# The output projection of a hybrid decoder layer by Strassen's algorithm, seven products of quarters instead of eight

## The chip, the core and the metric

The kernel runs on one core of a Trainium2 chip. The metric is the device time of one execution in microseconds (us). Within the core, TensorE (PE in the profile, its weight loads PEld) multiplies, VectorE (DVE), ScalarE (ACT) and GpSimd (POOL) do elementwise work, and the queue of SyncE (SP) issues every DMA of this kernel.

## What is computed

One decoder layer over 2048 tokens of width 2048: an input projection feeds a convolution branch and a windowed attention branch (each gated), their 1024 + 1024 channels are concatenated, and an output projection, a residual and a LayerNorm follow.

```python
proj = einsum("bsd,de->bse", x, w_in) + b_in
c_val, c_glu, c_gate, q, k, v, a_gate = split(proj)
y_conv = conformer_conv_branch(c_val, c_glu, ...) * silu(c_gate)   # GLU, causal conv of 31 taps, LayerNorm, swish
y_attn = swa_sink_attention(q, k, v, sinks) * silu(a_gate)         # window of 128, 16 heads, 2 kv heads
y = concatenate([y_conv, y_attn])
y = einsum("bse,ed->bsd", y, w_out) + b_out
out = layer_norm(2**0.25 * x + y, ln_g, ln_b)
```

All of it is float32. Each projection is made of three matmuls in a rounded 32-bit format: an operand is split into a rounded part (`hi`) and the remainder (`lo`), and `hi*hi + hi*lo + lo*hi` is summed (`mm3`).

## The kernel before

The tokens are worked in four chunks of 512 (`SC`, `NCH`). The body is one list of steps, 116 for each chunk: 8 "first" steps and 76 "in" steps (84 in all) for the input projection, with attention and convolution between them, then 32 "out" steps for the output projection. A step uses one weight tile of 128 x 1024 and gives PE 24 matmuls of 512 columns.

- Around each step, `load_w` fetches the raw weight tile three steps ahead (`wraw`, 3 buffers) and `split_w` splits it two steps ahead (`wspl`, 3 buffers): ACT makes `hi` (`copy`, L114), and `lo_part` (L117) makes the remainder on POOL for "in" steps and on DVE for "first" and "out" steps. A step's matmuls wait for both.
- Work of the convolution and of the LayerNorms waits in a deque (`bg`), from which `run_bg` takes some pieces in each step. At the first "out" step all that is left is run: the end of an inverse square root (`rsqrt_steps`) and eight `fin` pieces (L264 to L272), which make the convolution half of y.
- y is split into `hi` and `lo` where it is made: attention in pieces of 128 columns (`yah`, `yal`), the convolution in tiles of 512 (`ych`, `ycl`).
- An output column block `d` of 512 takes 8 steps. Four PSUM banks hold the four token rows of 128; `evac_out` adds each bank to the residual tile `xn` and feeds `bn_stats`. After the fourth block, `out_norm` queues 16 pieces for the final LayerNorm (ACT L435, DVE L436, POOL L437), which run in the next chunk's "first" steps. At the very end, `tail_norm` does it row by row.

A tile framework turns this into one instruction stream for each engine; it fills waiting time by its own estimate, so the order on an engine is not quite the order of the code. Each engine works its stream strictly in order.

Of the kernel before, what the change touches and what calls it, by code (L numbers as in the profile page):

```python
# [8 lines left out]
F32 = mybir.dt.float32  # L9
# [7 lines left out]
P = 128  # L17
# [13 lines left out]
NSLOT = 69  # L31
# [18 lines left out]
def hybrid_layer_kernel(ctx, tc, x, xT, w_first, w_in, w_out, consts, b_out, ln_g, ln_b, out):  # L50
# [9 lines left out]
    small = ctx.enter_context(tc.tile_pool(name="small", bufs=4))  # L60
    ps_acc = ctx.enter_context(tc.tile_pool(name="ps_acc", bufs=2, space=bass.MemoryType.PSUM))
# [87 lines left out]
    ys = {}  # L149
# [105 lines left out]
    def conv_var(c):  # L255
        ps = mean_bcast("vsplit", f"var{c}")
        v, y, tmp = slot(f"v{c}"), slot(f"rstd{c}"), slot(f"nt{c}")
        V.tensor_scalar(out=v, in0=ps, scalar1=EPS, scalar2=None, op0=ALU.add)
        bg.extend(rsqrt_steps(v, y, tmp))

        def fin(j):
            def f():
                a = st["conv", j]
                V.tensor_tensor(out=a, in0=a, in1=y, op=ALU.mult)  # L264
                u, t = half_silu_parts(a, half[:, 42 + j:43 + j], half[:, 50 + j:51 + j], f"cn{c}_{j}")
                silu_mul(u, u, t)
                bg_late.append((c, j, u))
                hi, lo = slot(f"ych{c}_{j}", F32R), slot(f"ycl{c}_{j}", F32R)
                V.tensor_tensor(out=u, in0=u, in1=st["gate", j], op=ALU.mult)
                copy(hi, u)  # L270
                lo_part(V, lo, u, hi)
                ys[c, 8 + j] = (hi, lo)  # L272
            return f
        bg_late = []
        bg.extend(fin(j) for j in range(8))
# [46 lines left out]
    def att_values(c, r, b):  # L322
        res = st.pop(("pm", r, b))
        pv = ps_pv.tile([P, 2, 256], F32, tag="pv", name=f"pv{c}_{r}_{b}")
        for kv in range(2):
            mv = slice(kv * 256, kv * 256 + 256)
            mm = []
            for n, (hi, lo) in enumerate(res):
                v = vt[:, b + 1 - n]
                mm.append((pv[:, kv, :], v[:, kv, :], hi[:, mv]))  # L330
                mm.append((pv[0:HD, kv, :], v[:, kv, 0:HD], lo[:, mv]))
            mm = [mm[0], mm[1], mm[3], mm[2]]
            for n, (o, l, m) in enumerate(mm):
                T.matmul(o, l, m, start=(n == 0), stop=(n == len(mm) - 1))  # L334

        o = small.tile([P, 2, P], F32, tag="o", name=f"o{c}_{r}_{b}")
        of = o.rearrange("p i q -> p (i q)")
        cols = slice(b * P, (b + 1) * P)
        for kv in range(2):
            rows, other = slice(kv * HD, (kv + 1) * HD), slice((1 - kv) * HD, (2 - kv) * HD)  # L340
            copy(of[rows], pv[other, kv, :])
            V.tensor_tensor(out=of[rows], in0=of[rows], in1=pv[rows, kv, :], op=ALU.add)
        for i in range(2):
            e = 2 * r + i
            if b == 0:
                ys[c, e] = (slot(f"yah{c}_{e}", F32R), slot(f"yal{c}_{e}", F32R))
            hi, lo = ys[c, e]
            V.tensor_tensor(out=o[:, i, :], in0=o[:, i, :], in1=st["ag", e][:, cols], op=ALU.mult)
            copy(hi[:, cols], o[:, i, :])
            lo_part(V, lo[:, cols], o[:, i, :], hi[:, cols])  # L350
# [56 lines left out]
    def evac_out(c, d, s, ps):  # L407
        z = st["z", c, s, d] = st["xn", s]
        V.tensor_tensor(out=z, in0=z, in1=ps, op=ALU.add)  # L409
        if d == 0:  # L410
            st["bn", c, s] = small.tile([P, 4, 6], F32, tag="bn", name=f"bn{c}_{s}", bufs=8)
        V.bn_stats(out=st["bn", c, s][:, d, :], in_=z)

# [29 lines left out]
    def out_norm(c):  # L443

        units = [(d, s) for d in range(4) for s in range(4)]

        def first():
            norm_small(c, range(4))
            load_gb(c, 0)

        def fin(n):
            def f():
                if n < 16:
                    d, s = units[n]
                    if s == 0 and d < 3:
                        load_gb(c, d + 1)
# [5 lines left out]
        return [first] + [fin(n) for n in range(18)]  # L462
# [3 lines left out]
    for c in range(NCH):  # L466
# [3 lines left out]
        for d in range(4):  # L470
            for p in range(8):
                steps.append(("out", c, d, p))
# [3 lines left out]
    def w_src(s):  # L476
        if s[0] == "first":
            return w_first[s[2]]
        return w_in[s[2] - 4, s[5]] if s[0] == "in" else w_out[s[2], s[3]]
# [10 lines left out]
    def split_w(n, parts=1, in_slots=False):  # L490
# [4 lines left out]
        eng = G if steps[n][0] == "in" else V  # L495
        if in_slots:
            hi, lo = ([slot(f"w{x}{n}_{i}", F32R) for i in range(2)] for x in "hl")
            parts = 2
        else:
            hi, lo = (wspl.tile([P, 1024], F32R, tag=f"w{x}", name=f"w{x}{n}") for x in "hl")  # L500
        for i in range(parts):
            w = slice(i * 1024 // parts, (i + 1) * 1024 // parts)
            h, l = (hi[i], lo[i]) if in_slots else (hi[:, w], lo[:, w])
            copy(h, t[:, w])
            lo_part(eng, l, t[:, w], h)
        splits[n] = (hi, lo) if in_slots else ((hi[:, 0:512], hi[:, 512:1024]), (lo[:, 0:512], lo[:, 512:1024]))
# [3 lines left out]
    per = 84 + 32  # L510
    for c in range(NCH):
# [10 lines left out]
        att.setdefault(base + 82, []).append((conv_var, c))  # L522

    ps = None

    def mm3(o, lh, ll, mh, ml, start, stop):
        T.matmul(o, lh, mh, start=start, stop=False)  # L527
        T.matmul(o, lh, ml, start=False, stop=False)  # L528
        T.matmul(o, ll, mh, start=False, stop=stop)  # L529

    def out_mm(c, n, p, i):
        hi, lo = splits[n]
        for kk in range(2):
            k = 2 * p + kk
            yh, yl = ys[c, k]
            cols = slice(i * P, (i + 1) * P)
            mm3(st["acc"][i], yh[:, cols], yl[:, cols], hi[kk], lo[kk], k == 0, k == KT - 1)
# [45 lines left out]
    split_x(0, 1)  # L583
    for n, s in enumerate(steps):
        c = s[1]
        tail = c == NCH - 1 and s[0] == "out" and s[2] == 3
        if c == 0 and s[0] == "first":
# [13 lines left out]
        elif tail:  # L601

            p = s[3]
            if p < 3:
                b = n - p
                if p == 0:
                    split_w(b + 2)
                for q in (2 * p + 3, 2 * p + 4):
                    if q < 8:
                        list(load_w(b + q))  # L610
                        split_w(b + q, in_slots=q < 5)
        else:
            list(load_w(n + 3))
            split_w(n + 2)
        for f, *args in att.get(n, []):
            f(*args)
        if s[0] == "first":
# [4 lines left out]
            for kk in range(2):  # L622
                k = 2 * p + kk
                xh, xl = xs[c, k]
                for t in range(4):
                    cols = slice(t * P, (t + 1) * P)
                    mm3(st["acc"][t], hi[kk][:, cols], lo[kk][:, cols], xh, xl, k == 0, k == KT - 1)
            if p == 7:
# [15 lines left out]
        else:  # L644
            _, c, d, p = s
            if d == 0 and p == 0:
                run_bg(len(bg))
            if p == 0:
                st["acc"] = four_banks(f"out{c}_{d}")
            if p == 2:  # L650
                st["bo"] = bcast_row(b_out, d, f"bo{c}_{d}")
            if 2 <= p < 6:
                xn = st["xn", p - 2] = slot(f"xn{c}_{d}_{p - 2}")
                r = c * SC + (p - 2) * P
                nc.sync.dma_start(out=xn, in_=x[r:r + P, d * 512:(d + 1) * 512])
            if 4 <= p:
                xn = st["xn", p - 4]
                V.scalar_tensor_tensor(out=xn, in0=xn, scalar=ALPHA, in1=st["bo"], op0=ALU.mult, op1=ALU.add)
            q = d * 8 + p
            if c + 1 < NCH and q >= 23:  # L660
                for k in (2 * (q - 23), 2 * (q - 23) + 1):
                    if k < KT:
                        load_x(c + 1, k)
                    if k >= 2:
                        split_x(c + 1, k - 2)
            if not tail:
                for i in range(4):
                    out_mm(c, n, p, i)
                if p == 7:
                    for i in range(4):  # L670
                        evac_out(c, d, i, st["acc"][i])
                    if d == 3:
                        bg.extend(out_norm(c))
            elif p < 3:
                for i in range(4):
                    out_mm(c, n, p, i)
            elif p == 7:
                for d2 in range(4):
                    load_gb(c, d2)
                for i in range(4):  # L680
                    for q in range(3, 8):
                        out_mm(c, n - 7 + q, q, i)
                    evac_out(c, d, i, st["acc"][i])
                    tail_norm(c, i)
        if not tail:
# [68 lines left out]
```

## Time and profile before

| | |
|---|---|
| median of 3 runs | 2746.8 us (2745.5 to 2747.04) |
| profiled execution | 2745.35 us, its span 2743.6 us |
| PE busy | 2696.2 us, 12448 matmuls |
| DVE / ACT / POOL busy | 1952.4 / 1120.5 / 1118.7 us |
| DMA | 308.53 MB, mean 112 GB/s |

The span is from the first instruction to the last. Matmuls overlap in the records: one of 512 columns shows about 390 ns, but the next starts about 227 ns later, and it is that distance that counts. The same holds in small for other engines. In rows of the timeline the first two numbers are the start and the length in us; in groups, "x304 | 746.7, 2459" means 304 instructions, 746.7 us together, 2459 ns for one on average.

### The profile page before, as it was taken

The page shows a single profiled execution, that of the slowest core. Times are in us where ns is not written, and L with a number is a line of the kernel's source. Part 1 is how long each engine was busy: PE and PEld are TensorE (multiplying, and loading weights), DVE is VectorE, ACT ScalarE, POOL GpSimd, SP SyncE. Part 2 cuts the span into 40 slices and gives each one's busy share as a digit, 9 for nine tenths or more (in the row PEclk, how much of TensorE's full clock was granted, in tenths as well). Part 3 has the DMA queues.
Part 4 walks back from the last instruction along what each step waited for, and adds up shares of the span by engine and source line. Part 5 has one row for each costly group of instructions (what it writes and reads, how often), then busy time and mean ns, then how long its engine had stood idle before and what let it go on. Part 6 is the DMA issues. An engine that isn't in the chain of part 4 may idle for free.

```text
span 2743.6 us, 33348 instructions
## 1 busy us (share of the span) xinstructions
PE 2696.2 (98%) x12448; PEld 2243.1 (82%) x12448; DVE 1952.4 (71%) x2986; ACT 1120.5 (41%) x2060; POOL 1118.7 (41%) x632
## 2 busy tenths in 40 slices
PE   9999999999999999999999999999999999999996
PEld 7888888888788888878878888887887888888885
DVE  5587877754857887775585779777457677986827
ACT  4344454522434445442243443544233345444422
POOL 2455555200645555610064555560006455556002
PEclk9999999999999999999999999999999999999998
DMA  5222222364422222235442222224544222222424
GB/s 179 96 89 85 79 91 92 100 208 145 148 91 92 85 78 93 85 129 189 142 153 87 90 77 85 92 86 147 171 150 146 85 92 85 77 92 86 158 99 142
DMA packets 101826, 308.53 MB, mean 112 GB/s; under 512 B 11296, under 2 KB 11424, under 8 KB 101664
## 3 DMA queue, kind: packets, MB, share of 16 engines
q1 hardware_dynamic: 101664, 306.40, 33.2%
q8 instruction: 98, 1.61, 0.2%
q14 instruction: 64, 0.52, 0.1%
HBM read 289.58 MB, written 16.78 MB: 112 GB/s over the span
## 4 chain that ended last, share of the span: by engine, by line
PE 90%; DVE 4%; issue 2%; ACT 2%; POOL 1%; DMA 1%; SPq 0%; DVEq 0%; POOLq 0%
PE in L529 21%; PE in L527 21%; PE in L528 21%; PE out L527 7%; PE out L529 7%; PE out L528 7%; PE pv L334 2%; PE sc L284 1%; PE sc L285 1%; PE pt L311 1%; POOL vsum L248 1%; DMA xn<-in_x_dram 1%; DVE wl L117 1%; DVE xn L436 0%; DVE xn L565 0%
## 5 line engine op out<-in xcount | busy, mean ns | idle before, releaser
L529 PE MATMUL in<-xh,wl 128*128 128x512 f32 x2688 | 1050.3, 391 | 10.9 <-DVE wl L117 10.9
L527 PE MATMUL in<-xh,wh 128*128 128x512 f32 x2688 | 1053.8, 392 | 5.6 <-ACT xh L114 5.6
L528 PE MATMUL in<-xl,wh 128*128 128x512 f32 x2688 | 1049.5, 390 | 0.0
L117 POOL TENSOR_TENSOR wl<-wr,wh 128x1024 fp32r<-128x1024 f32 x304 | 746.7, 2459 | 637.6 <-ACT wh L114 602.9
L114 ACT ACTIVATE wh<-wr 128x1024 fp32r<-128x1024 f32 (+1 forms) x467 | 488.6, 1050 | 824.8 <-PE out L529 345.8
L203 DVE SCALAR_TENSOR_TENSOR cv<-h,cst,cv 128x512 f32<-128x512 f32 x896 | 632.1, 746 | 2.3
L529 PEld LDWEIGHTS in<-xh,wl 128*128 128x128 f32 x2688 | 505.8, 188 | 119.1 <-DVE wl L117 12.6
L527 PEld LDWEIGHTS in<-xh,wh 128*128 128x128 f32 x2688 | 506.5, 188 | 106.2 <-ACT xh L114 5.6
L528 PEld LDWEIGHTS in<-xl,wh 128*128 128x128 f32 x2688 | 506.1, 188 | 101.6 <-DVE xl L117 0.5
L117 DVE TENSOR_TENSOR wl<-wr,wh 128x1024 fp32r<-128x1024 f32 (+1 forms) x163 | 214.1, 1316 | 255.3 <-ACT wh L114 250.7
L437 POOL TENSOR_TENSOR xn<-xn,b 128x512 f32<-128x512 f32 x48 | 85.8, 1819 | 582.9 <-DVE xn L436 582.9
L527 PE MATMUL out<-wh,yah 128*128 128x512 f32 x512 | 199.7, 391 | 4.0 <-DVE xn L409 4.0
L528 PE MATMUL out<-wl,yah 128*128 128x512 f32 x512 | 199.3, 389 | 0.0
L527 PE MATMUL out<-wh,ych 128*128 128x512 f32 x512 | 199.2, 389 | 0.0
L528 PE MATMUL out<-wl,ych 128*128 128x512 f32 x512 | 199.2, 389 | 0.0
L529 PE MATMUL out<-wh,ycl 128*128 128x512 f32 x512 | 199.2, 389 | 0.0
L529 PE MATMUL out<-wh,yal 128*128 128x512 f32 x512 | 198.6, 389 | 0.0
L299 ACT ACTIVATE pr<-pr,sm 128x128 f32<-128x128 f32 x256 | 99.8, 391 | 165.9 <-DVE sm L295 165.9
L527 PEld LDWEIGHTS out<-wh,yah 128*128 128x128 f32 x512 | 96.1, 188 | 27.1 <-DVE xn L409 6.3
L529 PEld LDWEIGHTS out<-wh,yal 128*128 128x128 f32 x512 | 96.1, 188 | 20.1
L529 PEld LDWEIGHTS out<-wh,ycl 128*128 128x128 f32 x512 | 96.1, 188 | 20.0
L527 PEld LDWEIGHTS out<-wh,ych 128*128 128x128 f32 x512 | 96.1, 188 | 20.0
(281 smaller groups left out, 2877.3 us busy)
## 6 DMA issues: line engine op xcount, KB each, us to landing
wr<-in_w_in_dram SPq DMA_DIRECT2D x304, 512.0 KB, 3.2
wr<-in_w_out_dram SPq DMA_DIRECT2D x128, 512.0 KB, 3.3
xr<-in_xT_dram SPq DMA_DIRECT2D x64, 256.0 KB, 4.1
xn<-in_x_dram SPq DMA_DIRECT2D x64, 256.0 KB, 5.8
out_dram<-xn SPq DMA_DIRECT2D x64, 256.0 KB, 2.1
wr<-in_w_first_dram SPq DMA_DIRECT2D x31, 512.0 KB, 3.7
bo<-in_b_out_dram SPq DMA_DIRECT2D x16, 256.0 KB, 5.9
g<-in_ln_g_dram SPq DMA_DIRECT2D x16, 256.0 KB, 5.4
```

What stands on the lines that cost most here:

```text
L114: A.activation(out=dst, in_=src, func=AF.Copy)
L117: eng.tensor_tensor(out=dst, in0=src, in1=hi.bitcast(F32), op=ALU.subtract)
L203: V.scalar_tensor_tensor(out=o, in0=h[:, t:t + SC], scalar=wt(t), in1=a, op0=ALU.mult, op1=ALU.add)
L248: G.tensor_tensor(out=s, in0=st["vsum"], in1=q, op=ALU.add)
L284: T.matmul(o, qs[:, b * P:(b + 1) * P], ks[kv][:, b * P:b * P + 256], start=True, stop=False)
L285: T.matmul(o, qs[:, b * P:(b + 1) * P], kl[kv][:, b * P:b * P + 256], start=False, stop=True)
L299: A.activation(out=p3[:, u, :], in_=p3[:, u, :], func=AF.Exp, scale=HD ** -0.5, bias=sm[:, 1, u:u + 1], accum_out=sm[:, 3, u:u + 1])
L334: T.matmul(o, l, m, start=(n == 0), stop=(n == len(mm) - 1))
L437: G.tensor_tensor(out=z, in0=z, in1=st["b", d], op=ALU.add)
L527: T.matmul(o, lh, mh, start=start, stop=False)
L528: T.matmul(o, lh, ml, start=False, stop=False)
L529: T.matmul(o, ll, mh, start=False, stop=stop)
```

## The change

The output projection of a chunk, 512 tokens x 2048 channels x 2048 columns, is cut into quarters (256 tokens, 1024 channels, 1024 columns; a is the attention half of y, b the convolution half) and done with seven products instead of eight, in the order `PRODS`. Each product takes 8 steps (two column blocks `dp`, four weight tiles `p`), so an "out" part has 56 steps instead of 32, but a step multiplies only 256 tokens, so it has 12 matmuls instead of 24.

```diff
-NSLOT = 69
+NSLOT = 63
+PRODS = (1, 2, 5, 6, 3, 7, 4)
-    wraw = ctx.enter_context(tc.tile_pool(name="wraw", bufs=3))
-    wspl = ctx.enter_context(tc.tile_pool(name="wspl", bufs=3))
+    wraw = ctx.enter_context(tc.tile_pool(name="wraw", bufs=4))
+    wspl = ctx.enter_context(tc.tile_pool(name="wspl", bufs=4))
...
+    def gen_y(c, i, k):
+        a, b = yr.get((c, k)), yr.get((c, 8 + k))
+        h1, h2 = slice(0, 256), slice(256, 512)
...
+        if i == 1:
+            src = a[:, h1]
+        elif i == 2:
+            src = b[:, h1]
+        elif i == 4:
+            src = b[:, h2]
+        elif i == 5:
+            G.tensor_tensor(out=sm, in0=a[:, h2], in1=b[:, h2], op=ALU.add)
+        elif i == 6:
+            G.tensor_tensor(out=sm, in0=sm, in1=a[:, h1], op=ALU.subtract)
+        elif i == 3:
+            G.tensor_tensor(out=sm, in0=b[:, h1], in1=sm, op=ALU.subtract)
+        else:
+            G.tensor_tensor(out=a[:, h1], in0=a[:, h1], in1=a[:, h2], op=ALU.subtract)
...
+        copy(t[:, 0, :], src)
+        lo_part(V, t[:, 1, :], src, t[:, 0, :])
...
+    def tsum_add(dp, p, kk):
+        b11, b12, b21, b22 = st["tb", dp, p, kk]
+        G.tensor_tensor(out=b11, in0=b12, in1=b11, op=ALU.subtract)
+        G.tensor_tensor(out=b12, in0=b22, in1=b12, op=ALU.subtract)
+        G.tensor_tensor(out=b22, in0=b22, in1=b11, op=ALU.subtract)
+        G.tensor_tensor(out=b21, in0=b21, in1=b22, op=ALU.subtract)
...
     def split_w(n, parts=1):
-        eng = G if steps[n][0] == "in" else V
+        eng = G if steps[n][0] == "in" or steps[n][0] == "out" and steps[n][4] % 2 else V
...
+    for j in range(16):
+        job = (j // 8, j // 2 % 4, j % 2)
+        att.setdefault(10 + 4 * j, []).append((tsum_load, *job))
+        att.setdefault(14 + 4 * j, []).append((tsum_add, *job))
+        att.setdefault(18 + 4 * j, []).append((tsum_store, *job))
...
-            list(load_w(n + 3))
-            split_w(n + 2)
+            list(load_w(n + 4))
+            split_w(n + 3)
...
+            if q == 0:
+                while len(bg) > 8:
+                    run_bg(1)
+                out_banks(c)
+            if i == 1 and dp == 0:
+                gen_y(c, 1, 4 + p)
...
+            out_mm(n, i, dp, p, (0,) if tail else (0, 1))
...
+            if p == 3 and not tail:
+                late = [(evac_out, c, i, dp, tp) for tp in range(2)]
+            if i == 1:
+                run_bg(1)
+            if i != 4:
+                gen_y(c, PRODS[PRODS.index(i) + 1], 4 * dp + p)
+            if q == 40:
+                bg.extend(out_norm(c, (0, 1)))
+            if q > 40 and not tail:
+                run_bg(1)
```

In the changed file `copy` is L117, `lo_part` L120, `fin` L268 to L272, `scale_xn` L410, `add_bank` L413, `bn_stats` L420, the four sums of `gen_y` L466 to L475, the LayerNorm pieces L531 to L533. In detail:

- **y** is kept unsplit (`yr`), and `gen_y` makes the operand of the next product one tile of 256 columns at a time: 56 tiles in a chunk, 32 of them with a sum on POOL first, each with a copy on ACT and a remainder on DVE. The splits of 128 columns in the attention are gone.
- **Weight sums**: four of the seven products need a sum of weight quarters. In the first chunk's "in" part, 16 jobs load weights, form the sums on POOL (64 subtractions of 512 columns) and store them in DRAM, from where all chunks load them as they load weights.
- **Weight splits** in the "out" part: 56 instead of 32 in a chunk, the remainder on DVE for even `p` and on POOL for odd `p`. Loads are issued four steps ahead, splits run three ahead, with four buffers each.
- **Banks**: two sets of four PSUM banks (X, the ones attention uses, and Z) take turns; every product is added to one output quarter when it is done, so there are 28 additions of a bank in a chunk (16 before), one product running on in its bank.
- **LayerNorm**: rows 0 and 1 are done from the sixth product on, rows 2 and 3 in the next chunk's "first" steps. At the end, only rows 2 and 3 go through `tail_norm`.

Where instructions stand now: on POOL, around the first chunk's "out" part (`wl` is a weight remainder, the number behind it the step, of which 84 is the first "out" step; `vsum` belongs to the convolution's LayerNorm, `xn` with `b` to the final one of the next "first" steps). Before:

```order
L248 TENSOR_TENSOR vsum0_5_4215<-vsum0_4_4175,sq0_5_4213 128x512
L248 TENSOR_TENSOR vsum0_6_4220<-vsum0_5_4215,sq0_6_4218 128x512
L248 TENSOR_TENSOR vsum0_7_4225<-vsum0_6_4220,sq0_7_4223 128x512
L117 TENSOR_TENSOR wl83_4265<-wr83_4231,wh83_4264 128x1024
L437 TENSOR_TENSOR xn0_0_0_4544<-xn0_0_0_4544,b0_0_5694 128x512
```

POOL goes from the last "in" weight straight to the LayerNorm of the next part. In the changed kernel, on POOL, from the split of out step 15 on (`S` are the sums for products 5, 6 and 3, `ya` that for 7):

```order
L120 TENSOR_TENSOR wl99_4976<-wr99_4951,wh99_4975 128x1024
L466 TENSOR_TENSOR S0_0_4901<-ya0_0_1241,cn0_0u_4649 128x256
L466 TENSOR_TENSOR S0_0_4901<-ya0_1_1243,cn0_1u_4682 128x256
L466 TENSOR_TENSOR S0_2_4946<-ya0_2_2140,cn0_2u_4714 128x256
L466 TENSOR_TENSOR S0_2_4946<-ya0_3_2142,cn0_3u_4746 128x256
L469 TENSOR_TENSOR S0_0_4901<-S0_0_4901,ya0_0_1241 128x256
L120 TENSOR_TENSOR wl101_5027<-wr101_5002,wh101_5026 128x1024
L466 TENSOR_TENSOR S0_4_4997<-ya0_4_2849,cn0_4u_4780 128x256
L466 TENSOR_TENSOR S0_4_4997<-ya0_5_2851,cn0_5u_4810 128x256
L469 TENSOR_TENSOR S0_0_4901<-S0_0_4901,ya0_1_1243 128x256
L469 TENSOR_TENSOR S0_2_4946<-S0_2_4946,ya0_2_2140 128x256
L469 TENSOR_TENSOR S0_2_4946<-S0_2_4946,ya0_3_2142 128x256
```

POOL now has work throughout the "out" part, and nearly all of its 32 sums stand between the splits of out steps 15 and 25, fourteen of them between those of steps 17 and 19 alone.

On DVE, in the stretch where the convolution half of y is made (`cn` the pieces of `fin`, `wl` the weight remainders). Before:

```order
L117 TENSOR_TENSOR ycl0_1_4408<-cn0_1u_4402,ych0_1_4407 128x512
L144 SCALAR_TENSOR_TENSOR cn0_2u_4413<-cn0_2t_4414,cn0_2u_4413 128x512
L269 TENSOR_TENSOR cn0_2u_4413<-cn0_2u_4413,cgate0_2u_3959 128x512
L117 TENSOR_TENSOR ycl0_2_4419<-cn0_2u_4413,ych0_2_4418 128x512
L117 TENSOR_TENSOR wl89_4573<-wr89_4536,wh89_4572 128x1024
L144 SCALAR_TENSOR_TENSOR cn0_3u_4424<-cn0_3t_4425,cn0_3u_4424 128x512
```

Now, at its end:

```order
L147 SCALAR_TENSOR_TENSOR cn0_7u_4868<-cn0_7t_4869,cn0_7u_4868 128x512
L271 TENSOR_TENSOR cn0_7u_4868<-cn0_7u_4868,cgate0_7u_4606 128x512
L120 TENSOR_TENSOR wl100_5005<-wr100_4973,wh100_5004 128x1024
L120 TENSOR_TENSOR y0_2_7_4874<-cn0_7u_4868,y0_2_7_4874 128x256
L120 TENSOR_TENSOR y0_5_0_4903<-S0_0_4901,y0_5_0_4903 128x256
L120 TENSOR_TENSOR y0_5_1_4925<-S0_0_4901,y0_5_1_4925 128x256
L413 TENSOR_TENSOR xn0_0_0_4634<-xn0_0_0_4634,out0_0_4883 128x512
```

The weight remainder of out step 16 (`wl100`) stands between the last pieces of the convolution, and right behind it DVE takes up the tiles that POOL's sums feed.

More of the change, by code (lines that the diff above doesn't have):

```diff
@@ L461, in fin @@
             return f
-        return [first] + [fin(n) for n in range(18)]
+        return [first] + [fin(n) for n in range(len(units) + 2)]
     steps = []
@@ L469, in hybrid_layer_kernel @@
             steps += [("in", c, t, *ORDER[t], hf) for hf in range(2)]
-        for d in range(4):
-            for p in range(8):
-                steps.append(("out", c, d, p))
+        steps += [("out", c, i, dp, p) for i in PRODS for dp in range(2) for p in range(4)]
     raws, splits = {}, {}
@@ L583, in hybrid_layer_kernel @@
     split_x(0, 1)
+    late = []
     for n, s in enumerate(steps):
         c = s[1]
-        tail = c == NCH - 1 and s[0] == "out" and s[2] == 3
         if c == 0 and s[0] == "first":
@@ L644, in hybrid_layer_kernel @@
         else:
[L645 to L684, printed above, removed]
@@ L685, in hybrid_layer_kernel @@
-        if not tail:
+            _, c, i, dp, p = s
+            q = 8 * PRODS.index(i) + 4 * dp + p
+            tail = c == NCH - 1 and q >= 52
+            if q == 0:
[4 more added lines that the diff above has]
+                gen_y(c, 1, 4 + p)
+            if i == 2 and dp == 0 and p == 0:
+                st["Z"] = four_banks(f"out{c}")
+            if i in NEW:
+                if p == 0:
+                    st["bo"] = bcast_row(b_out, NEW[i](dp, 0)[1], f"bo{c}_{i}_{dp}")
+                if p < 2:
+                    load_xn(c, *NEW[i](dp, p))
+                else:
+                    scale_xn(*NEW[i](dp, p - 2), st["bo"])
@@ new lines, in hybrid_layer_kernel @@
+            if c + 1 < NCH and q >= 39:
+                if q < 55:
+                    load_x(c + 1, q - 39)
+                if q >= 40:
+                    split_x(c + 1, q - 40)
+            if q == 55:
+                if not tail:
+                    bg.extend(out_norm(c, (2, 3)))
+                else:
+                    run_bg(len(bg))
+                    for d in range(4):
+                        load_gb(c, d)
+                    evac_out(c, i, dp, 0)
+                    tail_norm(c, 2)
+                    for pp in range(4):
+                        out_mm(n - 3 + pp, i, dp, pp, (1,))
+                    evac_out(c, i, dp, 1)
+                    tail_norm(c, 3)
@@ L686, in hybrid_layer_kernel @@
+        if not (s[0] == "out" and tail):
             raws.pop(n, None)
```

162 lines of the change are left out of this document (110 added, 52 removed).

## The prediction

> **What bounds the kernel now.** I read the page's busy shares first, then the chain that ended last.
>
> ```profile
> PE 2696.2 (98%) x12448; PEld 2243.1 (82%) x12448; DVE 1952.4 (71%) x2986; ACT 1120.5 (41%) x2060; POOL 1118.7 (41%) x632
> PE 90%; DVE 4%; issue 2%; ACT 2%; POOL 1%; DMA 1%; SPq 0%; DVEq 0%; POOLq 0%
> ```
>
> TensorE bounds it: 90% of the chain is its matmuls. Next the busy time by stage, to see who else works in the "out" parts; two of them, with the "in" part ahead of the first (the edges come from the PE timeline below):
>
> ```profile
> core 0: us, PE busy (x) PEld busy (x) DVE busy (x) ACT busy (x) POOL busy (x), PEclk, DMA share, GB/s
> 0.00:507.70 507.70, 500.57 (x2344) 417.88 (x2345) 367.86 (x589) 223.08 (x450) 257.75 (x161) 1.00 0.29 100
> 507.70:683.20 175.50, 174.62 (x769) 143.90 (x768) 100.93 (x132) 60.34 (x74) 0.00 (x0) 1.00 0.50 165
> 1186.80:1362.80 176.00, 175.19 (x773) 144.55 (x772) 101.48 (x133) 60.15 (x74) 0.00 (x0) 1.00 0.49 165
> ```
>
> An "out" part takes 175.5 us, PE is busy without a gap, DVE 101 us, and POOL does nothing at all. The timeline gives the matmul's pace:
>
> ```profile
> 507.73 0.39 PE L527 MATMUL out<-wh,yah 128*128 128x512 f32 x1
> 507.95 0.39 PE L528 MATMUL out<-wl,yah 128*128 128x512 f32 x1
> 683.02 0.39 PE L529 MATMUL out<-wh,ycl 128*128 128x512 f32 x1
> 683.25 0.39 PE L527 MATMUL in<-xh,wh 128*128 128x512 f32 x1
> ```
>
> From 507.73 to 683.25 it is 175.5 us for 768 matmuls, 0.228 each; a single distance is 0.227, which I use.
>
> **What is removed.** Seven products of 96 matmuls are 672 instead of 768 in a chunk: 96 x 0.227 = 21.8 us, 87 us in all four. The new "out" part could take 672 x 0.227 = 152.3 us. But a weight step now has 12 matmuls, 2.72 us, where it had 5.44, and each still needs its load, its copy on ACT and its remainder on DVE or POOL. So the question is whether the other engines can feed PE at twice the rate.
>
> **Prices of what is added.** From DVE's and POOL's timelines, each where the other engine was idle or on PSUM work:
>
> ```profile
> 505.52 1.22 DVE L117 TENSOR_TENSOR wl<-wr,wh 128x1024 fp32r<-128x1024 f32 x1
> 506.66 0.69 DVE L130 TENSOR_TENSOR nt<-nt,rstd 128x512 f32<-128x512 f32 x1
> 512.82 2.49 DVE L264 TENSOR_TENSOR conv<-conv,rstd 128x512 f32<-128x512 f32 x4
> 120.51 2.40 POOL L117 TENSOR_TENSOR wl<-wr,wh 128x1024 fp32r<-128x1024 f32 x1 [3.05 <-ACT wh L114]
> 128.80 1.31 POOL L117 TENSOR_TENSOR plu<-pmu,phu 128x512 fp32r<-128x512 f32 x1
> ```
>
> On DVE a remainder of 1024 columns takes 1.14 us from start to start, 512 columns 0.62; by that slope I estimate 0.35 for 256. POOL takes 2.40 and 1.30; by its slope 0.75 for 256. Busy time alone would fit: counting the changed "out" part of the first chunk in order, from behind the split of its first step to that of its last, DVE has 27 remainders of 1024, 70 operations of 512 with two inputs from SBUF and 56 of 256, so 30.8 + 43.4 + 19.6 = 93.8 us, and besides 36 operations on a bank or with one input (22 us by 0.62) and 18 small ones (3 us). POOL has 28 remainders, 32 sums and 8 LayerNorm additions: 67.2 + 24.0 + 10.4 = 101.6 us. ACT has 56 copies of 1024 by 1.05 us (row below), 56 of 256 that I put at 0.4 and some 30 others, about 100 us. Each is under 152.
>
> ```profile
> L114 ACT ACTIVATE wh<-wr 128x1024 fp32r<-128x1024 f32 (+1 forms) x467 | 488.6, 1050 | 824.8 <-PE out L529 345.8
> ```
>
> But DVE and POOL don't run side by side. The timeline of the LayerNorm behind the first "out" part, DVE first, then POOL, and two rows from a little earlier:
>
> ```profile
> 691.16 9.80 DVE L436 TENSOR_TENSOR xn<-xn,g 128x512 f32<-128x512 f32 x7
> 700.89 2.31 DVE L117 TENSOR_TENSOR wl<-wr,wh 128x1024 fp32r<-128x1024 f32 x1
> 703.12 9.16 DVE L436 TENSOR_TENSOR xn<-xn,g 128x512 f32<-128x512 f32 x6
> 712.20 2.28 DVE L117 TENSOR_TENSOR wl<-wr,wh 128x1024 fp32r<-128x1024 f32 x1
> 714.40 4.05 DVE L436 TENSOR_TENSOR xn<-xn,g 128x512 f32<-128x512 f32 x3
> 691.98 12.36 POOL L437 TENSOR_TENSOR xn<-xn,b 128x512 f32<-128x512 f32 x7 [192.82 <-DVE xn L436]
> 704.98 10.63 POOL L437 TENSOR_TENSOR xn<-xn,b 128x512 f32<-128x512 f32 x6 [0.63 <-DVE xn L436]
> 716.24 5.60 POOL L437 TENSOR_TENSOR xn<-xn,b 128x512 f32<-128x512 f32 x3 [0.63 <-DVE xn L436]
> 496.76 2.40 POOL L117 TENSOR_TENSOR wl<-wr,wh 128x1024 fp32r<-128x1024 f32 x1 [1.69 <-ACT wh L114]
> 497.66 2.58 DVE L117 TENSOR_TENSOR wl<-wr,wh 128x1024 fp32r<-128x1024 f32 x1 [1.20 <-ACT wh L114]
> ```
>
> The same DVE operation goes from 0.62 to 1.40 us, the remainder from 1.22 to 2.3, and POOL's addition from 1.30 to 1.77. From 691.16 to 718.4 (27.2 us) DVE did 16 x 0.62 + 2 x 1.14 = 12.2 us of work at its lone price and POOL about 14 additions, 18.4 us: together 30.6 in 27.2, a factor of 1.12 where two independent engines could reach 2. Near enough they take turns. Operations with one input in PSUM escape: the convolution's taps (L203) average 0.746 us although POOL is busy half of the "in" part.
>
> ```profile
> L203 DVE SCALAR_TENSOR_TENSOR cv<-h,cst,cv 128x512 f32<-128x512 f32 x896 | 632.1, 746 | 2.3
> 500.17 0.68 DVE L258 TENSOR_SCALAR v<-var 128x512 f32<-128x512 f32 x1
> ```
>
> **The "out" part, added up.** Where DVE's row above stands (500.17) the work counted here can begin, 7.6 us ahead of PE's first "out" matmul. At out step 25, behind POOL's block of sums, DVE must have done 12 remainders, 44 operations of 512 and 32 of 256 (13.7 + 27.3 + 11.2 = 52.2 us), POOL 13 remainders and all 32 sums (31.2 + 24.0 = 55.2): 107.4 / 1.12 - 7.6 = 88.3 us after PE's start, where PE alone would be there at 25 x 2.72 = 68.0. So PE comes 20.3 us late, and the part takes at least 152.3 + 20.3 = 172.6. At the last step the sum is (93.8 + 101.6) / 1.12 - 7.6 = 166.9 against 149.6, with DVE's other 25 us all hidden in POOL's turns; with none hidden 192.1, so 42.5 late and 194.8. I take 182, four tenths of the way: a third of that other work stands ahead of step 25, where POOL has a backlog to hide it; the rest doesn't, and the streams are in strict order. That is +6.5 us a chunk against 175.5, **+26** in all (-12 to +77): Strassen's 87 us are spent before they are earned.
>
> **The rest, part by part.**
>
> The LayerNorm moved: today its 16 pieces delay a "first" step's remainder, and PE waits in three of the four chunks. PE's rows, and its windows:
>
> ```profile
> 710.68 0.39 PE L528 MATMUL in<-xl,wh 128*128 128x512 f32 x1
> 714.53 0.73 PE L529 MATMUL in<-xh,wl 128*128 128x512 f32 x1 [3.47 <-DVE wl L117]
> 712.00:714.00 2.00, 0.00 (x0) 1.00 0.35 131
> 716.00:718.00 2.00, 2.00 (x6) 0.50 0.89 261
> PE in L529 <- DVE wl L117: 10.9, 4, 3.5
> ```
>
> 3.85 us without a matmul, then some seven at half the clock, about 5 us a time. Eight pieces instead of 16, and splits one step further ahead, should end much of it; but the backlog of the "out" part falls there. **-8** (-15 to 0).
>
> The tail: PE's last matmul and DVE's last chains of a row:
>
> ```profile
> 2722.16 0.39 PE L529 MATMUL out<-wh,ycl 128*128 128x512 f32 x1
> 2721.10 0.68 DVE L409 TENSOR_TENSOR xn<-xn,out 128x512 f32<-128x512 f32 x1
> 2730.47 0.67 DVE L409 TENSOR_TENSOR xn<-xn,out 128x512 f32<-128x512 f32 x1
> ```
>
> Now 21.2 us pass from PE's end to the span's end, since four rows pass through DVE at 9.4 us each. With two rows, the first starts 5.4 us (24 matmuls) before PE's end, the second 9.4 later, and it needs the 13.1 from 2730.47 to 2743.6: 17.1. **-4** (-6 to +1).
>
> The weight sums: 64 x 1.30 = 83 us of POOL in a part of 507.7 us where it is busy 257.75, so 67%. Their stores sit in SP's queue ahead of weight loads and wait for POOL, but loads run four steps, 21 us, ahead. **+2** (0 to +15).
>
> At nothing: the split of y taken out of the attention (it lies under the "in" matmuls, and the list of PE's waits doesn't name it), and the banks' changes of hands, since each is emptied three steps before its next product.
>
> DMA: an "out" part moves 56 x 0.524 MB of weights and 56 pieces of 0.262 MB (16 of the next chunk's x, 16 of the residual, 8 of the bias, 16 of the LayerNorm's factors and results), 44 MB. The busiest stretch of today:
>
> ```profile
> 544.00:564.00 20.00, 19.11 (x84) 15.35 (x83) 16.72 (x25) 4.05 (x5) 0.00 (x0) 1.00 0.92 299
> ```
>
> 299 GB/s at a share of 0.92 is 325 at most, so 44 MB need 135 us: hidden on average. In the last two products it is 18.4 MB, 57 us, against 43.5 of PE; since PE is late by then and half of these loads are not urgent, I add nothing and keep it as a rival.
>
> Sum: +26 - 8 - 4 + 2 = +16, so 2745.35 + 16 = **2761 us**. (That execution is 1.5 us under the median of the runs shown.)
>
> **Rivals.**
>
> *Faster: the turns matter less.* POOL's sums begin in gaps that the block count misses and DVE's bank work fills POOL's turns. If PE waits only for the convolution's last pieces, some 5 us, a part takes 158: 4 x (158 - 175.5) = -70, -10 as above: 2665. Half as good (168): -30 - 10: 2705. For it: two operations in 27 us do overlap, the rate is a mean. Against: the counts at step 25 leave no slack. It decides once a part ends less than 24 us late, under 176.5 us.
>
> *Slower: full exclusion.* If POOL's and DVE's operations exclude each other for their whole length, the last step comes at 195.4 - 7.6 = 187.8, 38 late, a part takes 190.5, and the sum is +60 - 10: 2795. For it: the two rows at 496.76, where the remainder on DVE ended 3.5 us after POOL's began, the sum of both alone. The Trainium skill states this as the rule ("SBUF — State Buffer", "Who interferes with whom"): the port pair shared by VectorE and GpSimd is an exclusive lock, held for the instruction, against DVE operations with two SBUF inputs; by it the total would be this rival's 2795. The LayerNorm rows above, with their 1.12, stand slightly better than that rule.
>
> *Slower: the clock.* Each wait as long as the 3.85 us above costs another 1.7 at half clock. If the 20 to 30 us of lateness come as five such waits in a part: +8.5 x 4 on the forecast: 2795.
>
> *Slower: DMA.* If the last two products run at 57 us instead of the forecast's 48: +36: 2797.
>
> **How the numbers follow.** Changes within 0.2% (5.5 us) can't be told from none. Forecast, 2751 to 2785: 0.25. Full exclusion 0.20, clock 0.07, DMA 0.05: slower 0.57. The faster rival as far as 2705: 0.20, beyond, to 2665: 0.15, so 0.35. Between them, unchanged: 0.08. The range leaves out about 0.12 below 2695 and 0.08 above 2835; the forecast's own range is 2712 to 2838 by the terms' bounds.
>
> **What would show it.** Right: "out" parts of 175 to 190 us; POOL busy over half of them; two-input DVE operations near 1.2 us where they took 0.69; PE waiting for a POOL remainder around out step 19 to 25. Wrong: parts near 155 us with PE gapless, or waits of PE on DMA. The step most likely to fail is the factor 1.12 and how much of DVE's other work it hides.

## The result, and the profile after

| | before | after |
|---|---|---|
| median (lowest to highest) | 2746.91 us (2745.5 to 2747.04) | 2817.57 us (2816.29 to 2821.37) |
| ratio, 95% interval | | 1.0261 (1.0243 to 1.0278): slower by 2.6% |
| profiled execution, its span | 2745.35, 2743.6 us | 2818.5, 2816.8 us |
| the four "out" parts (the last to PE's last matmul) | 175.5, 175.3, 176.3, 175.3 us | 199.8, 197.3, 199.0, 192.7 us |

The product has 384 matmuls less, and yet the kernel is 71 us slower. The page of after, its busy shares:

```profile
PE 2665.3 (95%) x12064; PEld 2183.6 (78%) x12064; DVE 2218.8 (79%) x3120; ACT 1242.2 (44%) x2220; POOL 1635.7 (58%) x938
```

PE's share fell from 98 to 95%: it waits now. The busy time of two "out" parts, in the columns of the prediction's rows:

```profile
508.80:708.60 199.80, 168.93 (x674) 130.44 (x673) 181.56 (x207) 98.80 (x148) 119.52 (x67) 0.95 0.63 213
1209.20:1406.50 197.30, 168.79 (x674) 131.26 (x673) 180.95 (x208) 99.67 (x148) 119.50 (x67) 0.94 0.64 217
```

DVE (third) is busy for 181.6 us of 199.8, so 91%. But by the prediction's count and its lone prices it had 93.8 + 25 = 118.8 us of work: by that estimate 63 us of its "busy" time are waiting inside instructions. POOL (fifth) had 101.6 us of work and shows 119.5, so it waits for 18. PE is fed by both. By shape in the same stretch, first DVE, then POOL (the last two numbers ahead of the second bar are the group's busy time and one operation's ns):

```profile
L120 DVE TENSOR_TENSOR wl<-wr,wh 128x1024 fp32r<-128x1024 f32 x27 | 41.1, 1523 | 2.2 <-ACT wh L117 2.2
L120 DVE TENSOR_TENSOR y<-S,y 128x256 fp32r<-128x256 f32 x24 | 24.2, 1032 | 1.8 <-ACT y L117 1.8
L532 DVE TENSOR_TENSOR xn<-xn,g 128x512 f32<-128x512 f32 x8 | 10.9, 1372 | 0.3 <-ACT xn L531 0.3
L420 DVE BATCH_NORM_STATS2 bn<-xn 128x6 f32<-128x512 f32 x14 | 9.0, 677 | 0.0
L413 DVE TENSOR_TENSOR xn<-xn,out 128x512 f32<-128x512 f32 x12 | 7.7, 676 | 0.6 <-PE out L629 0.6
L120 POOL TENSOR_TENSOR wl<-wr,wh 128x1024 fp32r<-128x1024 f32 x27 | 74.1, 2748 | 75.8 <-ACT wh L117 75.8
```

The pieces of y (256 columns, two inputs from SBUF) take 1032 ns on average, the sum with a bank (`xn<-xn,out`) and the statistics the usual 676. PE's waits, the five largest in the "out" parts:

```profile
PE out L628 <- POOL wl L120: 26.8, 11, 4.8
PE xb L628 <- DVE wl L120: 16.9, 15, 2.3
PE xa L627 <- ACT y L117: 16.1, 8, 3.6
PE xa L628 <- DVE wl L120: 10.5, 7, 2.8
PE xa L628 <- POOL wl L120: 10.2, 9, 2.4
```

The first row is the wait that the prediction placed near out step 19. Here it is on the timelines of PE, DVE and POOL:

```profile
578.46 0.39 PE L627 MATMUL out<-wh,y 128*128 128x512 f32 x1
583.65 0.50 PE L628 MATMUL out<-wl,y 128*128 128x512 f32 x1 [4.80 <-POOL wl L120]
584.68 0.63 PE L628 MATMUL out<-wl,y 128*128 128x512 f32 x1
587.25 0.55 PE L628 MATMUL out<-wl,y 128*128 128x512 f32 x1
579.66 1.74 DVE L120 TENSOR_TENSOR wl<-wr,wh 128x1024 fp32r<-128x1024 f32 x1
581.32 2.56 DVE L120 TENSOR_TENSOR y<-S,y 128x256 fp32r<-128x256 f32 x1
573.77 4.18 POOL L475 TENSOR_TENSOR ya<-ya 128x256 f32<-128x256 f32 x4
580.28 3.31 POOL L120 TENSOR_TENSOR wl<-wr,wh 128x1024 fp32r<-128x1024 f32 x1
```

POOL works off sums until 580, then its remainder takes 3.31 us instead of 2.40; DVE's remainder ends at 581.4, and from there on it is 2.2 us. DVE's next piece, 0.35 us by itself, takes 2.56: it ends at 583.9, 0.3 behind POOL's remainder. PE stands still for 5 us, and then its matmuls come 0.43 us apart until 587.6 instead of 0.227.

Lateness of PE, at some steps of the first "out" part, against 2.72 us a step from the part's first matmul (read from PE's timeline, which holds all 672 matmuls of this part, 12 a step):

| step | 8 | 16 | 24 | 32 | 40 | 48 | 54 |
|---|---|---|---|---|---|---|---|
| after | 9.8 | 16.0 | 27.8 | 33.6 | 33.6 | 43.5 | 47.4 |

It rises in two stretches: through the convolution's last pieces and the sums (to step 32), and again at the end, where the LayerNorm pieces run.

### The profile page after: what moved, and what is told of

It reads as the page before. It is cut to its first block, busy times and chain, and to the rows that moved or that the text cites. A ratio compares the mean times of both kernels' runs of the same rounds, so it can differ in the third digit from the quotient of the medians.

```text
span 2816.8 us, 34054 instructions
## 1 busy us (share of the span) xinstructions
PE 2665.3 (95%) x12064; PEld 2183.6 (78%) x12064; DVE 2218.8 (79%) x3120; ACT 1242.2 (44%) x2220; POOL 1635.7 (58%) x938
## 3 DMA queue, kind: packets, MB, share of 16 engines
q1 hardware_dynamic: 140832, 402.88, 42.3%
## 5 line engine op out<-in xcount | busy, mean ns | idle before, releaser
L120 POOL TENSOR_TENSOR wl<-wr,wh 128x1024 fp32r<-128x1024 f32 x416 | 1052.8, 2533 | 857.2 <-ACT wh L117 817.5
L117 ACT ACTIVATE wh<-wr 128x1024 fp32r<-128x1024 f32 (+1 forms) x561 | 587.5, 1053 | 678.6 <-PE in L628 350.0
L120 DVE TENSOR_TENSOR wl<-wr,wh 128x1024 fp32r<-128x1024 f32 (+1 forms) x145 | 215.7, 1490 | 30.8 <-ACT wh L117 30.5
L628 PE MATMUL out<-wl,y 128*128 128x512 f32 x384 | 156.2, 409 | 28.1 <-POOL wl L120 26.8
L627 PE MATMUL out<-wh,y 128*128 128x512 f32 x384 | 155.2, 406 | 11.6 <-DVE xn L413 5.7
L629 PE MATMUL out<-wh,y 128*128 128x512 f32 x384 | 154.1, 405 | 8.1 <-DVE y L120 8.1
L533 POOL TENSOR_TENSOR xn<-xn,b 128x512 f32<-128x512 f32 x56 | 103.2, 1864 | 76.4 <-DVE xn L532 58.7
L378 DVE SCALAR_TENSOR_TENSOR q<-in,cst,q 64x512 fp32r<-64x512 f32 x64 | 48.0, 750 | 100.7 <-ACT q L377 98.1
L628 PE MATMUL xa<-wl,y 128*128 128x512 f32 x256 | 104.8, 410 | 20.9 <-DVE wl L120 10.5
L120 POOL TENSOR_TENSOR plc<-pmc,phc 128x512 fp32r<-128x512 f32 x64 | 85.2, 1331 | 62.1 <-ACT phc L117 62.0
L627 PE MATMUL xa<-wh,y 128*128 128x512 f32 x256 | 104.8, 409 | 16.1 <-ACT y L117 16.1
L628 PEld LDWEIGHTS out<-wl,y 128*128 128x128 f32 x384 | 75.1, 196 | 50.6 <-POOL wl L120 31.8
L629 PE MATMUL xa<-wh,y 128*128 128x512 f32 x256 | 104.2, 407 | 7.3 <-DVE y L120 7.3
L120 POOL TENSOR_TENSOR plu<-pmu,phu 128x512 fp32r<-128x512 f32 x64 | 83.5, 1304 | 38.3 <-ACT phu L117 37.0
```

The costliest lines, as they stand in the source:

```text
L117: A.activation(out=dst, in_=src, func=AF.Copy)
L120: eng.tensor_tensor(out=dst, in0=src, in1=hi.bitcast(F32), op=ALU.subtract)
L378: V.scalar_tensor_tensor(out=qs[other], in0=ps[rows], scalar=b1[rows], in1=qs[rows].bitcast(F32), op0=ALU.add, op1=ALU.subtract)
L533: G.tensor_tensor(out=z, in0=z, in1=st["b", d], op=ALU.add)
L627: T.matmul(o, lh, mh, start=start, stop=False, skip_group_check=free)
L628: T.matmul(o, lh, ml, start=False, stop=False, skip_group_check=free)
```

## The experiments

Theories: (E) POOL's operations and DVE's two-input operations exclude each other for their whole length, so that their lone prices add up; (D) DMA; (S) something of DVE's own stream, such as its order or its number of operations. Each kernel is the changed one with the edit shown, except the last two, and "part" is an "out" part. Runs without an interval were measured once; the kernel before took 2746 to 2748 us (medians) beside them on the same chips.

**no_sums**: the products take unsummed tiles of y in place of POOL's 32 sums; all else stays.

```diff
-            G.tensor_tensor(out=sm, in0=a[:, h2], in1=b[:, h2], op=ALU.add)
-            src = sm
+            src = a[:, h2]
...
```

> The 32 sums of gen_y on POOL in each out part are left out (the seven products then multiply unsummed tiles). An out part took 199 us in the changed kernel, PE's floor is 152. Theory (DVE's operations with two SBUF inputs and POOL's operations exclude each other for their whole length, and the sum of both sets the part): POOL's 101.6 us fall to 77.6, the last step comes at 93.8 + 77.6 - 7.6 = 163.8 us, and with the 9 us by which the changed kernel stood above this sum a part takes about 175 us, the whole about 2720. Rival 1 (DVE's own stream is too long, POOL doesn't matter): DVE's stream is the same, so 195 to 199 us a part, about 2817. Rival 2 (DMA): the same bytes, so 199.

2770.32 us, parts of 187.9, 188.4, 183.7 and 181.1. The lateness at step 24 fell from 28 to 16, so the block of sums counts, but a part lost 12 us on average where 24 us of POOL work went, and the 175 that E gave were missed by 9 to 13 in the first three. DVE's busy time fell to 169.7, so it still waited for 51 us with 77.6 us of POOL work left. The sums are part of the cause, the smaller one.

**w_dve**: all remainders of the "out" steps on DVE.

```diff
-        eng = G if steps[n][0] == "in" or steps[n][0] == "out" and steps[n][4] % 2 else V
+        eng = G if steps[n][0] == "in" else V
```

> All weight remainders of the out parts go to DVE, none to POOL; POOL keeps the sums. Theory (exclusion): DVE's two-input work is 93.8 + 28 x 1.14 = 125.7 us, POOL's 34.4, last step at 125.7 + 34.4 - 7.6 = 152.5, so a part of about 164 us and a whole of about 2677: faster although DVE gets 32 us more to do. Rival 1 (DVE's own stream is too long): 32 us longer than 199, so about 225 us a part and a whole above 2900. Rival 2 (DMA): 199 us a part.

2715.36 us, 1.2% below the kernel before, the first three parts 172.3 to 172.5. DVE took on 31.9 us of work and was busy for less:

```profile
508.00:680.50 172.50, 159.17 (x674) 126.69 (x673) 160.25 (x227) 97.40 (x146) 60.84 (x40) 0.98 0.69 235
```

160.25 against 150.7 us of work: it waits for 9.5 beside 34.4 us of POOL work in short pieces. S, which gave 225 us a part, is refuted; the expectation of 164 was 8 too low.

**sums_dve**: the sums on DVE, the remainders divided.

```diff
-            G.tensor_tensor(out=sm, in0=a[:, h2], in1=b[:, h2], op=ALU.add)
+            V.tensor_tensor(out=sm, in0=a[:, h2], in1=b[:, h2], op=ALU.add)
... (the other three likewise)
```

> The 32 sums go to DVE, POOL keeps half of the weight remainders. Theory (exclusion): DVE 93.8 + 32 x 0.35 = 105.0, POOL 77.6, last step at 175.0, a part of about 187 us, a whole of about 2768. Rival 1 (DVE's own stream): 11 us longer than 199, about 210, a whole of about 2860. Rival 2 (DMA): 199.

2795.63 us, parts of 190 to 194: 5 to 9 us less than after in three of them and 3 in the last, in the direction that E gives and half of its size.

**all_dve**: both edits; POOL is left with the LayerNorm additions.

> Both at once: weight remainders of the out parts and sums on DVE, POOL keeps only the LayerNorm's additions there. Theory (exclusion): DVE's two-input work 136.9, POOL 10.4; what remains is DVE's own stream, 136.9 + 25 of other work = 162 us, less the 7.6 of lead, so a part of 158 to 168 us and a whole of 2665 to 2700, under the 2747 of the kernel before. Rival 1 (DVE's own stream sets it already): 43 us longer than 199 a part, a whole of about 2990. Rival 2 (DMA): 199 us a part, 2817.

2703.59 us, ratio to before 0.9839 (0.9822 to 0.9855); the first three parts 169 to 172, 1 to 4 us above what E gave. By shape on DVE:

```profile
L120 DVE TENSOR_TENSOR wl<-wr,wh 128x1024 fp32r<-128x1024 f32 x54 | 67.7, 1255 | 0.4 <-ACT wh L117 0.4
L120 DVE TENSOR_TENSOR y<-S,y 128x256 fp32r<-128x256 f32 x24 | 9.8, 414 | 0.6 <-ACT y L117 0.5
```

The pieces of y are back at 414 ns from 1032, and 54 remainders on DVE alone cost it 67.7 us where 27 beside POOL's 27 cost it 41.1 and the pieces 14 more. That is E's mechanism by itself. PE is 5.3 us late from step 24 to 48 and then loses another 11, in a stretch where the DMA share is 1.03:

```profile
650.00:660.00 10.00, 6.88 (x29) 4.74 (x28) 9.96 (x15) 5.53 (x8) 3.58 (x2) 1.00 1.03 381
```

DVE is 100% busy there too, and POOL has two LayerNorm additions: DMA or DVE? Two runs ask this.

**half_dma** and **all_dve_half_dma** (after and all_dve): the "out" steps load half of each weight tile and use it twice; the operations keep their sizes.

```diff
+            if steps[n][0] == "out":
+                w = slice(0, 512)
...
+                src = t[:, 0:512].unsqueeze(1).broadcast_to([P, 2, 512])
```

> The changed kernel with half of the weight bytes: each out step loads only the first 512 columns of its weight tile and uses them twice (so the product is that of other weights). Bytes of an out part fall from 44 MB to about 29. Theory (exclusion of DVE and POOL): DVE and POOL do the same, so about 197 us a part, within 4 us of the 199 (a little less where the last two products wait for x and weights); the whole 2800 to 2817. Rival (DMA paces the part): the last two products, which grow late by 13 us, and the waits for weights go, a part of 180 to 185 us, the whole about 2750.

> The version with everything on DVE (2703.6 us, a part 169.5 us, 17 late: 6 by step 24, flat to step 48, 10 at the end), with half the weight bytes as above. If DMA sets the lateness at the end (its share is 1.0 from 650 to 670 us): a part of about 160 us, the whole about 2667. If DVE's own stream sets it (busy all of that time, with the LayerNorm's pieces and POOL's additions beside them): 168 to 170 us, the whole 2697 to 2705.

all_dve_half_dma took 2700.96 us, and PE begins its last step 15.8 us late (16.1 with full weights). That speaks against DMA at the end of the part, but doesn't settle it: from 650 to 670 us the DMA share was still 0.93 and 0.85, at 281 and 276 GB/s instead of 381 and 335. late_norm, below, settles it. half_dma took 2845.28 us, parts of 200 to 205, which neither theory gave. Less traffic didn't help (in its first part a DMA share of 0.47 and 151 GB/s). Besides, the shorter parts of w_dve and late_norm move nearly the bytes of after's 199.8 us (40.5 and 39.3 MB, 42.6 in after) at higher rates, so DMA doesn't pace the part, and D is refuted. Why half_dma got worse by 28 us is open; in its "out" parts PE waits for POOL's remainders for 67.0 us in all, where it waits for 46.4 in after. It isn't a clean halving: POOL's stream was planned in another order, with a wait for a convolution piece ahead of a remainder that the changed kernel's POOL doesn't have in this part:

```profile
551.86 2.38 POOL L120 TENSOR_TENSOR wl<-wr,wh 128x1024 fp32r<-128x1024 f32 x1 [5.11 <-DVE cn_5u L271]
```

**late_norm**: all_dve, and the LayerNorm of all four rows in the next chunk's "first" steps, as in the kernel before (the last chunk as in the changed one).

```diff
-            if q == 40:
+            if q == 40 and c == NCH - 1:
                 bg.extend(out_norm(c, (0, 1)))
-            if q > 40 and not tail:
+            if q > 40 and c == NCH - 1 and not tail:
                 run_bg(1)
...
-                    bg.extend(out_norm(c, (2, 3)))
+                    bg.extend(out_norm(c, (0, 1, 2, 3) if c < NCH - 1 else (2, 3)))
```

> Everything on DVE, and the LayerNorm of all four row blocks in the next chunk's steps as in the kernel before (only the last chunk keeps rows 0 and 1 in its out part). That takes 8 DVE multiplications, POOL's only work and 16 DMAs out of the end of an out part. If the 10 us at the end come from DVE with POOL or from DMA: a part of about 160 us for three chunks, and up to 4 us of new waits in a first part: the whole 2675 to 2690. If neither: 2700 to 2710.

**2676.76 us, ratio to before 0.9741 (0.9725 to 0.9757)**, the fastest version. In the first part the lateness stays at 5.4 us from step 24 to the end, parts take 157.7, 159.0, 160.3 and 163.0. So it was the LayerNorm pieces; whether by DVE's multiplications or by POOL's additions isn't separated. The first part's window, and ten of its last us:

```profile
509.90:667.60 157.70, 154.24 (x674) 125.55 (x673) 153.64 (x243) 97.82 (x142) 0.00 (x0) 1.00 0.72 249
650.00:660.00 10.00, 10.00 (x46) 8.29 (x45) 9.71 (x14) 5.45 (x8) 0.00 (x0) 1.00 0.98 370
```

PE is busy for 98% of the part and DVE for 97%, at full clock and with POOL idle. In its last 17 us the DMA share is 0.98 and 1.01, and PE doesn't wait: the 11 us that all_dve lost there weren't DMA. Strassen's product is earned, and DVE has next to no time left.

**late_norm_split**: the changed kernel with the same late LayerNorm, remainders and sums left divided.

> This is the changed kernel with one edit: the LayerNorm of all four rows runs in the next chunk's first steps (the last chunk as it was), while the remainders stay divided between DVE and POOL and the sums stay on POOL. If the LayerNorm pieces at the end of a part cost what they cost with all the work on DVE (lateness at the last step 15.9 against 6.3 us), three parts fall by about 10 us, from 199 to about 189, and the whole to about 2788. If the late end in the changed kernel is only DVE's backlog from the turns with POOL, the pieces add less: parts of 194 or more and 2803 to 2818.

2781.3 us, parts of 187.4, 187.1, 186.1 and 191.7. The LayerNorm pieces cost 10 to 13 us in each of three parts (PE's lateness at step 54 of the first is 35.1 instead of 47.4). For the rest, 187 against late_norm's 158, the code of the two kernels differs only in which engine makes 28 remainders and 32 sums of a part: 104.5 us between them.

**pool_short**: POOL's remainders in four pieces of 256 columns.

```diff
-            lo_part(eng, lo[:, w], t[:, w], hi[:, w])
+            k = 4 if eng is G and steps[n][0] == "out" else 1
+            for j in range(w.start, w.stop, 1024 // parts // k):
+                v = slice(j, j + 1024 // parts // k)
+                lo_part(eng, lo[:, v], t[:, v], hi[:, v])
```

> This is the changed kernel with each weight remainder that POOL makes for an out step cut into four operations of 256 columns, about 0.75 instead of 2.40 us each, so 3.0 a remainder and some 16 us more of POOL work in a part. If every microsecond of POOL's work is taken from DVE, whatever its pieces, a part becomes up to 16 us longer: about 205 to 215, the whole 2840 to 2880. If what DVE loses is set by the length of the POOL operation that it meets, short pieces let it in between: DVE waits less than the 63 us of a part in the changed kernel, and a part takes 185 to 195, the whole 2760 to 2800.

2845.76 us, parts of 208.6, 204.1, 205.3 and 196.9. The first part's window, then one group of POOL and one of DVE:

```profile
509.90:718.50 208.60, 176.05 (x674) 135.04 (x673) 164.26 (x206) 97.97 (x147) 143.99 (x148) 0.91 0.60 203
```

```profile
L120 POOL TENSOR_TENSOR wl<-wr,wh 128x256 fp32r<-128x256 f32 x108 | 102.5, 980 | 63.2 <-ACT wh L117 63.2
L120 DVE TENSOR_TENSOR y<-S,y 128x256 fp32r<-128x256 f32 x24 | 17.9, 769 | 4.6 <-ACT y L117 4.6
```

Short pieces do let DVE in: its piece of y waits less (769 ns against 1032), and its waiting in the part is 164.3 - 118.8 = 45 us instead of 63. But POOL's own is 144.0 - 118.4 = 26 instead of 18 (four pieces by 0.75 make its work 16.8 us longer, 118.4). In its "out" parts PE waits for POOL's remainders for 42.3 us in all (46.4 in after) and for DVE's for 44.5 (28.7). So the length of a POOL operation shifts the waiting between the engines, and the part got longer with the sum of the work, as the first of the two expectations had it.

**before_pool**: the kernel before, with half of its "out" remainders on POOL.

```diff
-        eng = G if steps[n][0] == "in" else V
+        eng = G if steps[n][0] == "in" or steps[n][0] == "out" and steps[n][3] % 2 else V
```

> The kernel before with one edit: the weight remainders of odd p in the out parts go to POOL, as in the changed kernel. DVE's work at its lone price falls from 101 to about 83 us a part, POOL gets 38. Theory (exclusion): DVE waits for POOL, some 0.6 us for each us of POOL's work as in the changed kernel (63 of 101.6), so DVE's busy time is about 105 instead of 83, but a step lasts 5.44 us and PE doesn't notice: 175 to 177 us a part, the whole 2745 to 2750. Rival (a POOL remainder is late by itself, whatever DVE does): PE waits at odd steps here too, over 180 us a part, the whole over 2765.

2762.47 us, 14 above the kernel before, parts of 179.0 to 179.5: between the two expectations. With twice the time for a weight step there is room for the remainders, but the convolution's last pieces get late, one DVE piece of 0.69 us takes 2.88, and PE waits for the copy that follows:

```profile
PE out L527 <- ACT ych L114: 9.2, 4, 2.3
```

```profile
L144 DVE SCALAR_TENSOR_TENSOR cn_0u<-cn_0t,cn_0u 128x512 f32<-128x512 f32 x1 | 2.9, 2879 | 0.0
```

**All parts against one count.** With E, a part is what two-input DVE work and POOL work add up to, less the 7.6 us of head start, plus the last step's 2.7 (not under PE's 152.3). DVE's other 25 us can lie in POOL's turns or not: two bounds.

| kernel | two-input DVE + POOL, us | bounds of a part | measured (first three) |
|---|---|---|---|
| after | 93.8 + 101.6 | 190.5 to 215.5 | 197 to 200 |
| late_norm_split | 88.8 + 91.2 | 175.1 to 200.1 | 186 to 187 |
| no_sums | 93.8 + 77.6 | 166.5 to 191.5 | 184 to 188 |
| sums_dve | 105.0 + 77.6 | 177.7 to 202.7 | 190 to 194 |
| pool_short | 93.8 + 118.4 | 207.3 to 232.3 | 204 to 209 |
| w_dve | 125.7 + 34.4 | 155.2 to 180.2 | 172 |
| all_dve | 136.9 + 10.4 | 152.3 to 167.4 | 169 to 172 |
| late_norm | 131.9 + 0 | 152.3 | 158 to 160 |

The count holds for the first six (pool_short 3 us under its lower bound at most); where DVE alone sets the pace, parts lie 2 to 8 us above it. How much of the 25 us is hidden varies from all (pool_short) to 3 us (no_sums), and nothing here predicts that. The bounds are 25 us wide: half_dma, with the work of after and parts of 204 to 205, lies inside them as well.

## Why the prediction was right or wrong

The direction and its mechanism were right: PE can't be fed, because DVE and POOL take turns. The size was wrong: 2817.6 against 2761, a loss of 71 us where 16 was the sum. Of the signs named for "right", POOL's share and the wait near step 19 came, but no part fell in the 175 to 190 us. The terms, from the two profiles (before to after):

| term | predicted | measured |
|---|---|---|
| "out" parts | +26 | +86 (24.3 + 22.0 + 22.7 + 17.4) |
| LayerNorm and "first" waits | -8 | -10 |
| tail | -4 | -4 (21.2 to 17.4 us) |
| weight sums in the first "in" part | +2 | +1 |
| span | +16 | +73 |

- **The step that failed is the factor 1.12.** It came from a 27-us stretch in which 0.62-us operations of DVE met 1.30-us additions of POOL. At the place where it was used, the remainder of step 25 ends on POOL 96.4 us after PE's start, as the row below shows with the part's first matmul at 508.83:

```profile
602.67 2.57 POOL L120 TENSOR_TENSOR wl<-wr,wh 128x1024 fp32r<-128x1024 f32 x1
```

  So 107.4 us of counted work took 96.4 + 7.6 = 104.0: a factor of 1.03, not 1.12. PE came to this step about 28 us late, where 20.3 was forecast and 31.8 would be full exclusion.
- **"Four tenths of the way" came out, by luck.** The last step began 197 us after the first, where exclusion alone gives 187.8: 9 of DVE's other 25 us weren't hidden, and the forecast had put 9.4 on its lower bound of 172.6. No row fixed that share, and by the table above other versions hid anything from 3 us to all of it. With a factor of 1 in place of 1.12 the lower bound is the last step's, 190.5, and the same choice gives 190.5 + 9.4 = 199.9 us a part, and a sum of 4 x 24.4 - 10 = +88. Why the LayerNorm stretch overlapped more than the "out" part was not tried.
- **The rival "full exclusion"** had the right cause and stopped at 2795, since it hid all of that other work. The rule of the Trainium skill quoted there ("SBUF — State Buffer", "Who interferes with whom") agrees with these runs better than the 1.12 that I preferred to it: in the row at 581.32, a 0.35-us operation waits out a 2.4-us one.
- **The rival "DMA"** is refuted by the parts of w_dve and late_norm, shorter at a higher DMA rate. **The clock** has a part: behind its longer waits PE's matmuls were up to 0.43 us apart, which adds up to 12 us of the first part's 47 us of lateness, more than that rival's 8.5. What it costs in the end isn't separated: while DVE sets the pace, PE would wait anyway.
- **The rival "faster"** (parts of 158) is what late_norm reached, with the contention gone and the LayerNorm elsewhere.
- **The LayerNorm moved**: the gain was right, half of its reason wasn't. late_norm_split has all 16 pieces in the "first" steps of the later chunks again, and its "in" parts take the same 500.6 us as the changed kernel's (504 before): it isn't the number of pieces. What remains of my reasons is the splits one step further ahead, which wasn't tried alone. And the pieces that moved into the "out" part cost 10 to 13 us there, which the sum held only as part of the turns.
- **Weight sums, tail, banks**: as forecast. PE's longest wait for a bank is 1.4 us.

## What to carry to other kernels

Where DVE's two-input operations and POOL fill a stage together, add up their lone times as if they were one engine, and compare that sum with PE's time in the stage; the busy shares of the page hide it, since waiting inside an instruction counts as busy. "Dividing" such work between the two loses twice when POOL takes 2.40 us for what DVE does in 1.14: give it to DVE, and look for a stage with slack for what is not urgent. A saving in matmuls is earned only as far as the engines that feed them keep pace: here the same seven products cost 2.6% or gained 2.6%, by the placing of 60 remainders and sums and of eight LayerNorm pieces a chunk.

## What the runs showed that I had not expected

- Short DVE operations suffer most: 128x256 went from 414 to 1032 ns on average beside POOL's work (up to 2.62 us), the 1024-column remainder only from 1255 to 1523.
- Cutting POOL's operations shorter moved the waiting from DVE to POOL and won nothing (DVE 63 to 45 us, POOL 18 to 26).
- One DVE operation shows the turns by itself. A step of an inverse square root, on 2 columns and with one input, takes 0.17 us where POOL is idle (717.52), 2.32 where it starts 0.1 us behind a POOL remainder, and 0.66 in pool_short, where that POOL operation is 0.74 long; both times it ends 0.03 us behind that POOL operation. In after, then in pool_short:

```profile
658.80 2.40 POOL L120 TENSOR_TENSOR wl<-wr,wh 128x1024 fp32r<-128x1024 f32 x1 [7.77 <-ACT wh L117]
658.91 2.32 DVE L125 TENSOR_SCALAR w<-w 128x2 int32<-128x2 int32 x1
717.52 0.17 DVE L125 TENSOR_SCALAR w<-w 128x2 int32<-128x2 int32 x1
667.42 0.74 POOL L120 TENSOR_TENSOR wl<-wr,wh 128x256 fp32r<-128x256 f32 x1 [5.19 <-ACT wh L117]
667.53 0.66 DVE L125 TENSOR_SCALAR w<-w 128x2 int32<-128x2 int32 x1
```

  So two inputs aren't the only case; which operations with one input wait was not sorted out.
- Half the weight traffic came with 28 us more time in one kernel, which is not explained, and with none in the other (2700.96 us, where all_dve took 2701.2 to 2705.1).
